# Moving the softmax reciprocals and the near-bias copies from VectorE to GpSimd

## The chip, the cores and the metric

The kernel runs on one core of a Trainium2 chip. A core has five engines with a queue of instructions each: TensorE (PE in the profile; its weight loads are PEld), VectorE (DVE), ScalarE (ACT), GpSimd (POOL) and SyncE (SP), which issues DMA transfers. An engine works through its queue in order. If its next instruction waits for a semaphore, everything behind it waits too.

The metric is the device time of one execution in microseconds, as the median of the runs.

## The reference

Two layers of the same kind, on 1024 positions with 1024 channels. Each layer normalises its input, projects it, runs a convolution branch and a sparse-attention branch side by side, gates both, concatenates them and projects them out. The attention branch is the part that matters here:

```
cq = rmsnorm(c_q); q = (cq @ w_uq) -> 8 heads of 128; kv = rmsnorm(c_kv)      # one kv head for all
score = sum over index heads of w_idx * relu(q_idx @ k_idx)                   # causal
sel = top_k(score, 256)                                                       # keys for each query
logits = q . kv[sel] * 128**-0.5 + rel_bias[bucket(t - s)]
probs = softmax(logits where t - s >= 0)
o = (probs @ kv[sel]) @ w_uv;  y_attn = o * silu(g_attn)
y = concat(y_conv, y_attn) @ w_out;  x = x + gate * rmsnorm(y)
```

Input and output are float32, and TensorE products are made of three passes over high and low parts.

## The kernel before

The kernel doesn't gather the selected keys. It computes the logits of all causal keys and adds a mask with a very large number where a key isn't selected; the mask is the bfloat16 tile mask. The signs are turned: the logits come out of TensorE negated, and Exp is taken with scale −1, so the row maximum of the logits is a row minimum in the code.

The work order of the attention is a list, ORDER, of 16 runs (pr, c). pr is a pair of heads (0 to 3), c a pair of query tiles of 128 rows (0 to 3). A run handles two heads e and two tiles i = 2c, 2c + 1; tile i has 128 (i + 1) keys. There are 64 such tiles in a layer, 128 in all. One tile passes through these steps:

1. TensorE: logits lg (L116 to L118) into one of four PSUM buffers.
2. GpSimd: the near bias plus the mask into the last 256 columns of p (L846). For the tiles i < 2, where no key is masked but those of the future, there is no sum: GpSimd makes the causal triangle of the last 128 columns (L843, an affine_select), and for i = 1 a plain copy of the bias fills the 128 columns before (L842). The bias tile tb is ja or jv for some heads.
3. VectorE: lg plus the bias or the mask into p, with the row minimum mx in the same instruction (L852, L856).
4. ScalarE: Exp on p, with its row sum into ri[:, 0] (L859).
5. The reciprocal of the sum into ri[:, 1] (L860).
6. The scaling of p by it: on ScalarE (L862) for the runs of pr 0 and for (1, 0), 20 tiles of a layer, on GpSimd (L864) for the other 44.
7. For c < 3, TensorE transposes p into PSUM (pt, L877), and ScalarE (L882) and VectorE (L884) copy the result to SBUF in turn. For c = 3, VectorE transposes blocks (stage, L895) and DMAs through DRAM do the rest (pd, L898 and L907).
8. TensorE: value products av (L927); VectorE multiplies by the gate (L918).

p has five buffers (tag t4). A new tile's first writer on p (L842, L843 or L846) therefore waits until the transposes or the stage of the tile five before have read it.

The selection runs into the start of the attention: select(j) makes the mask of one of the six tiles with more than 256 keys. Its steps are a compare with count (L614), the number still needed (L616), an equality (L618), a scan (L619) and a product (L620) on VectorE, a sum on GpSimd (L621, gt) and the scaled mask on ScalarE (L622). The table SELECT places four of the six between runs of the first pairs.

The end of the attention carries other work: the loads of the output projection's weights (DMA raw, ScalarE woh L136, GpSimd wol L137) and the splitting of the attention's result into yh (ScalarE L993) and yl (VectorE or GpSimd, L994). Output projection matmuls o (L116 to L118) follow, some of them ahead of the last value products.

A scheduler with its own plan of durations fixes the order in which each engine gets its instructions; some edges are set by hand (issue_after). The order can therefore change in places that the edit doesn't touch.

The GpSimd instruction that the change uses exists elsewhere: L301 and L1051 compute x to the power −0.5 with tensor_tensor and op pow, against a tile mhalf of −0.5.

Of the kernel before, what the change touches and what calls it, by code (L numbers as in the profile page):

```python
# [11 lines left out]
F32 = mybir.dt.float32  # L12
# [7 lines left out]
OP = mybir.AluOpType  # L20
# [3 lines left out]
P = 128  # L24
# [56 lines left out]
def hybrid_kernel(ctx: ExitStack, tc: tile.TileContext, x, cT, w_ada, w_mod, bcol, bgate, g_pre, w_in, w_cp,  # L81
# [3 lines left out]
    V, S, G, T = nc.vector, nc.scalar, nc.gpsimd, nc.tensor  # L85

    cst = ctx.enter_context(tc.tile_pool(name="cst", bufs=1))
# [14 lines left out]
    def st(tag, shape, dt=F32, name=None, bufs=None):  # L102
        return sb.tile(shape, dt, name=name or tag, tag=tag, bufs=bufs or BUFS.get(tag, 1))
# [7 lines left out]
    def lg_ps(name="lg"):  # L111
        return ps.tile([P, 512], F32, name=name, tag="lg", bufs=4)

    def mm3(o, a, b, first, last):
        (ah, al), (bh, bl) = a, b
        T.matmul(o, ah, bh, start=first, stop=False)  # L116
        T.matmul(o, ah, bl, start=False, stop=False)  # L117
        return T.matmul(o, al, bh, start=False, stop=last)  # L118
# [28 lines left out]
    make_identity(nc, ident)  # L147
    mhalf = cst.tile([P, 16], F32, name="mhalf")
    V.memset(mhalf, -0.5)
    kc1 = cst.tile([P, 6], F32, name="kc1")  # L150
    kc2 = cst.tile([P, 6], F32, name="kc2")
    for j in range(6):
# [151 lines left out]
    def pieces(i):  # L304

        w = P * (i + 1)
        if i == 4:
            return [(0, 384), (384, 640)]
        return [(c, min(c + 512, w)) for c in range(0, w, 512)]
# [497 lines left out]
    def attention(l, cq, kv, v, mk, sga, wq, select, yc):  # L807
# [19 lines left out]
        def probs(q, tb_, i, early):  # L827

            w = P * (i + 1)
            o = []  # L830
            for c0, c1 in pieces(i):
                o.append((lg_ps("lg"), c0, c1))
                mark[2] = mm3(o[-1][0][:, :c1 - c0], tuple(x_[:, 128 * i:128 * i + 128] for x_ in q),
                              tuple(x_[:, c0:c1] for x_ in kv), True, True)
            n0 = max(0, w - 256)
            nw = w - n0
            tb = tb_[:, 256 - nw:]
            p = st("t4", [P, 1024], name="p")
            nb = p[:, n0:w]
            if i < 2:  # L840
                if nw > 128:
                    V.tensor_copy(nb[:, 0:nw - 128], tb[:, 0:nw - 128])  # L842
                G.affine_select(nb[:, nw - 128:nw], tb[:, nw - 128:nw], pattern=[[-1, P]],  # L843
                                compare_op=OP.is_ge, fill=BIG, base=0, channel_multiplier=1)
            else:
                G.tensor_tensor(nb, tb, mk[:, OFF[i] + n0:OFF[i] + w], op=OP.add)  # L846
            m = st("mx", [P, 3], name="mx", bufs=8)
            lo = FMAX
            for o_, c0, c1 in o:
                if c0 < n0:  # L850
                    e = min(c1, n0)
                    V.tensor_tensor_reduce(out=p[:, c0:e], in0=o_[:, :e - c0], in1=mk[:, OFF[i] + c0:OFF[i] + e],  # L852
                                           scale=1.0, scalar=lo, op0=OP.add, op1=OP.min,
                                           accum_out=m[:, c0 // 384:c0 // 384 + 1])
                    lo = m[:, c0 // 384:c0 // 384 + 1]
            mark[3] = V.tensor_tensor_reduce(out=nb, in0=o_[:, n0 - c0:w - c0], in1=nb, scale=1.0, scalar=lo,  # L856
                                             op0=OP.add, op1=OP.min, accum_out=m[:, 2:3])
            ri = st("ri", [P, 2], name="ri", bufs=8)
            mark[0] = S.activation(p[:, :w], p[:, :w], AF.Exp, scale=-1.0, bias=m[:, 2:3], accum_out=ri[:, 0:1])  # L859
            V.reciprocal(ri[:, 1:2], ri[:, 0:1])  # L860
            if early:
                S.activation(p[:, :w], p[:, :w], AF.Copy, scale=ri[:, 1:2])  # L862
            else:
                mark[1] = G.tensor_scalar(p[:, :w], p[:, :w], ri[:, 1:2], 1.0, op0=OP.mult, op1=OP.mult)  # L864
            return p
# [65 lines left out]
        def run(pr, c):  # L931

            if c == 3:
                if "pd" not in held:
                    held["pd"] = st("score", [P, 4, 2, 4, 4, 32], name="pd")
                pts = [[held["pd"][:, 2 * e + h] for h in range(2)] for e in range(2)]
            else:
                pts = [[st("hq", [P, 4, 256], name="pt") for _ in range(1 + c // 2)] for e in range(2)]
            for e in range(2):
                for ii in range(2):  # L940
                    i = 2 * c + ii
                    p = probs(*q[2 * pr + e], i, pr == 0 or (pr, c) == (1, 0))
                    if c == 3:
                        turned(p, ii, pts[e])
                    else:
                        transposed(p, i, ii, pts[e])
                for j in SELECT.get((pr, c, e), ()):
                    with tc.issue_after(mark[3].ins):
                        select(j)
            if back:  # L950
                back.pop()()
            for w in open_:
                w[0] += c + 1
            if open_ and open_[0][0] >= 3:
                values(*open_.pop(0)[1], mark[2])
            if c == 3:
                open_.append([0, (pr, c, pts)])
            else:
                values(pr, c, pts)
# [351 lines left out]
```

## Time and profile before

| | |
|---|---|
| median of 3 runs | 1219.5 us (1219.34 to 1225.55) |
| profiled execution, its own time | 1223.55 us |
| its span, first to last instruction | 1221.8 us |
| mean granted TensorE clock | 0.984 of full speed |
| TensorE busy | 1151.2 us, 94% |
| VectorE busy | 910.9 us, 75% |
| ScalarE busy | 704.4 us, 58% |
| GpSimd busy | 567.1 us, 46% |

The profiled execution is 4.05 us above the median, and 1.75 us of it lie around the span. Times below are from the span's start. The attention of layer 0 lies at about 360 to 540 us, that of layer 1 at about 950 to 1130 us.

How to read the views: a busy row of a stretch gives how long each engine worked in it. A row of waits names the engine and line that waited, behind the arrow the engine, tile and line whose end released it, then the total, the number of times and the longest. A timeline row gives start and duration, engine, line and operation, out<-in with shapes, and in brackets how long the engine had been idle before it and what ended that. Matmuls overlap, so a TensorE row's duration is longer than its share of the pace.

### The profile page before, as it was taken

To read this page: it belongs to the slowest core of one execution; us is meant where nothing else is said; L and a number is where in the kernel's file an instruction comes from. 1 tells how busy PE (TensorE), PEld (TensorE's weight loads), DVE (VectorE), ACT (ScalarE), POOL (GpSimd) and SP (SyncE) were. 2 spreads that over 40 slices of the span, in tenths; PEclk is the share of its full clock that TensorE was granted. 3 is DMA by queue.
4 is the path that set the end of the run, shared out by engine and by line. 5 is a ranking of instruction groups with operands and counts; after the bars stand their busy time and mean duration, and the time that the engine had idled before them with its cause. 6 is when DMAs were issued, how large, how long until landed. Compare 5 with 4: busy or idle time off the path is not lost. (4 is left out here: it accounts for less than half of the span.)

```text
span 1221.8 us, 23105 instructions
## 1 busy us (share of the span) xinstructions
PE 1151.2 (94%) x7592; PEld 954.0 (78%) x7592; DVE 910.9 (75%) x2214; ACT 704.4 (58%) x1624; POOL 567.1 (46%) x1178
## 2 busy tenths in 40 slices
PE   6999999999998799999999999999999788998998
PEld 3788888877875467689988888888788566676997
DVE  4667798898877778857686588898888888777315
ACT  4545767766875645552354457786577575466221
POOL 3441226547543355664492411454665345576322
PEclk9999999999998999999999999999999898999999
DMA  9630258852110155658761220986111005567205
GB/s 351 206 86 18 69 178 268 278 195 79 34 38 1 24 156 155 186 195 264 262 212 31 57 52 20 288 293 198 55 36 45 9 1 139 138 162 217 89 18 190
DMA packets 145384, 161.68 MB, mean 132 GB/s; under 512 B 63080, under 2 KB 116848, under 8 KB 145264
## 3 DMA queue, kind: packets, MB, share of 16 engines
q1 hardware_dynamic: 145264, 160.21, 42.9%
q8 instruction: 60, 0.98, 0.4%
q14 instruction: 60, 0.49, 0.1%
HBM read 130.79 MB, written 29.37 MB: 131 GB/s over the span
## 5 line engine op out<-in xcount | busy, mean ns | idle before, releaser
L563 DVE TENSOR_SCALAR_CACHE_REDUCE jv<-pl,cand 128x768 int8<-128x768 uint16 (+1 forms) x186 | 187.9, 1010 | 31.6 <-POOL cand L570 20.7
L558 ACT ACTIVATE ja<-pl,cand 128x896 int8<-128x896 uint16 (+1 forms) x186 | 154.2, 829 | 63.9 <-POOL cand L570 49.3
L859 ACT ACTIVATE p<-p,mx 128x128 f32<-128x128 f32 (+7 forms) x128 | 98.3, 770 | 62.3 <-DVE mx L856 59.9
L116 PE MATMUL o<-woh,yh 128*128 128x256 f32 x384 | 109.1, 286 | 0.2 <-DVE mx L856 0.2
L117 PE MATMUL o<-wol,yh 128*128 128x256 f32 x384 | 108.0, 283 | 0.0
L118 PE MATMUL o<-woh,yl 128*128 128x256 f32 x384 | 107.6, 283 | 0.0
L137 POOL TENSOR_TENSOR wul<-raw,wuh 128x342 fp32r<-128x342 f32 (+1 forms) x48 | 47.0, 1003 | 129.6 <-ACT wuh L136 123.5
L116 PE MATMUL u<-hT,wuh 128*128 128x512 f32 x256 | 101.4, 396 | 0.0
L116 PE MATMUL g<-hT,wgh 128*128 128x512 f32 x256 | 101.2, 395 | 0.0
L118 PE MATMUL u<-hT,wul 128*128 128x512 f32 x256 | 100.0, 391 | 0.0
L117 PE MATMUL u<-hT,wuh 128*128 128x512 f32 x256 | 100.0, 391 | 0.0
L117 PE MATMUL g<-hT,wgh 128*128 128x512 f32 x256 | 99.8, 390 | 0.0
L118 PE MATMUL g<-hT,wgl 128*128 128x512 f32 x256 | 99.7, 390 | 0.0
L494 DVE SCALAR_TENSOR_TENSOR score<-relu,widx,score 128x384 f32<-128x384 f32 (+2 forms) x84 | 78.9, 977 | 18.7 <-ACT relu L486 18.1
L486 ACT ACTIVATE relu<-ixs 128x512 f32<-128x512 f32 (+2 forms) x140 | 66.7, 523 | 35.9 <-PE ixs L480 35.4
L864 POOL TENSOR_SCALAR p<-p,ri 128x384 f32<-128x384 f32 (+3 forms) x88 | 67.8, 777 | 37.1 <-DVE ri L860 36.8
L1036 ACT ACTIVATE ja<-o 128x256 int8<-128x256 f32 x64 | 24.5, 383 | 99.3 <-PE o L118 99.3
L480 PE MATMUL ixs<-ix 128*128 128x512 f32 (+2 forms) x320 | 76.3, 356 | 0.5 <-ACT relu L486 0.5
L116 PEld LDWEIGHTS o<-woh,yh 128*128 128x128 f32 x384 | 73.1, 191 | 2.4 <-issue 1.2
L117 PEld LDWEIGHTS o<-wol,yh 128*128 128x128 f32 x384 | 73.3, 191 | 0.3 <-issue 0.3
L118 PEld LDWEIGHTS o<-woh,yl 128*128 128x128 f32 x384 | 72.9, 191 | 0.0
L927 PE MATMUL av<-pt,v 128*64 128x256 f32 (+1 forms) x384 | 61.0, 371 | 9.1 <-DVE pt L884 5.3
(312 smaller groups left out, 3460.4 us busy)
## 6 DMA issues: line engine op xcount, KB each, us to landing
wt<-in_wl_dram SPq DMA_DIRECT2D x64, 512.0 KB, 6.0
wa<-in_w_mod_dram SPq DMA_DIRECT2D x32, 512.0 KB, 4.8
pd<-stage SPq DMA_DIRECT2D x192, 64.0 KB, 1.9
pd<-pd SPq DMA_DIRECT2D x48, 256.0 KB, 3.1
raw<-in_w_in_dram SPq DMA_DIRECT2D x64, 171.0 KB, 2.6
wa<-in_w_ada_dram SPq DMA_DIRECT2D x16, 512.0 KB, 10.1
raw<-in_w_out_dram SPq DMA_DIRECT2D x32, 171.0 KB, 3.5
raw<-in_w_in_dram SPq DMA_DIRECT2D x32, 170.0 KB, 2.6
```

Source lines behind the costliest of these rows:

```text
L116: T.matmul(o, ah, bh, start=first, stop=False)
L117: T.matmul(o, ah, bl, start=False, stop=False)
L118: return T.matmul(o, al, bh, start=False, stop=last)
L137: eng.tensor_tensor(lo[:, c:e], raw[:, :e - c], f32(hi[:, c:e]), op=OP.subtract)
L480: mark = T.matmul(o[:, :c1 - c0], s_[:, 128 * i:128 * i + 128], ix[:, kk, c0:c1], start=kk == 0, stop=kk == 1)
L486: S.activation(r[:, c0:c1], o[:, :c1 - c0], AF.Relu)
L494: V.scalar_tensor_tensor(acc, r[:, :w], wc, acc, op0=OP.mult, op1=OP.add)
L558: S.activation(ja[:, :wid(j)], src, AF.Sign, scale=-1.0, bias=col(cand, c), accum_out=col(ct_, c))
L563: V.tensor_scalar(jv[:, :wid(j)], src, col(cand, c), None, op0=OP.is_lt, op1=OP.add, accum_out=col(ct_, c))
L859: mark[0] = S.activation(p[:, :w], p[:, :w], AF.Exp, scale=-1.0, bias=m[:, 2:3], accum_out=ri[:, 0:1])
L864: mark[1] = G.tensor_scalar(p[:, :w], p[:, :w], ri[:, 1:2], 1.0, op0=OP.mult, op1=OP.mult)
L927: T.matmul(o[64 * e:64 * e + 64, 128 * ii:256], lh, pt[:, ii:2, :, j % 4, :] if c == 3 else pt[:, j % 4, 128 * ii:256], start=j == 0, stop ...
```

## The change

A constant tile mone, 128x1 with −1.0, is set once on VectorE. The copy L842 and the reciprocal L860 are issued on GpSimd; the reciprocal becomes x to the power −1, a tensor_tensor with op pow against mone. The steps before and after them stay where they are. New line numbers are two higher.

```diff
     mhalf = cst.tile([P, 16], F32, name="mhalf")
     V.memset(mhalf, -0.5)
+    mone = cst.tile([P, 1], F32, name="mone")
+    V.memset(mone, -1.0)
...
             if i < 2:
                 if nw > 128:
-                    V.tensor_copy(nb[:, 0:nw - 128], tb[:, 0:nw - 128])
+                    G.tensor_copy(nb[:, 0:nw - 128], tb[:, 0:nw - 128])
                 G.affine_select(nb[:, nw - 128:nw], tb[:, nw - 128:nw], pattern=[[-1, P]],
                                 compare_op=OP.is_ge, fill=BIG, base=0, channel_multiplier=1)
...
             mark[0] = S.activation(p[:, :w], p[:, :w], AF.Exp, scale=-1.0, bias=m[:, 2:3], accum_out=ri[:, 0:1])
-            V.reciprocal(ri[:, 1:2], ri[:, 0:1])
+            G.tensor_tensor(ri[:, 1:2], ri[:, 0:1], mone[:, 0:1], op=OP.pow)
```

128 reciprocals and 16 copies change engines. Because the scheduler plans anew, other instructions move as well. In the orders below each row is an instruction with line, operation, tiles and shape.

VectorE in the early stretch of layer 0, before, around the near-bias copy of p<-jv and the selects of 640 and 768 columns:

```order
L842 COPY p<-ja 128x128
L860 RECIPROCAL ri<-ri 128x1
L884 COPY pt<-pt 128x2x128
L860 RECIPROCAL ri<-ri 128x1
L842 COPY p<-jv 128x128
L614 TENSOR_SCALAR gt,cnt<-score,tf 128x640
L618 TENSOR_SCALAR eq<-score,tf 128x640
L614 TENSOR_SCALAR gt,cnt<-score,tf 128x768
L884 COPY pt<-pt 128x2x128
L618 TENSOR_SCALAR eq<-score,tf 128x768
L820 SCALAR_TENSOR_TENSOR q_4534<-uq,q_4533 128x512
```

The same place after the change (L616 is the old L614, L620 the old L618, L886 the old L884):

```order
L886 COPY pt<-pt 128x2x128
L616 TENSOR_SCALAR gt,cnt<-score,tf 128x640
L620 TENSOR_SCALAR eq<-score,tf 128x640
L616 TENSOR_SCALAR gt,cnt<-score,tf 128x768
L620 TENSOR_SCALAR eq<-score,tf 128x768
L886 COPY pt<-pt 128x2x128
L822 SCALAR_TENSOR_TENSOR q_4536<-uq,q_4535 128x512
```

The compares and equalities of both selects now follow the first copy of pt directly, and both equalities stand ahead of the second.

GpSimd in the same stretch, before, from the sums of the selects of 384 and 512 columns on:

```order
L621 TENSOR_TENSOR gt<-gt,eq 128x384
L621 TENSOR_TENSOR gt<-gt,eq 128x512
L843 AFFINE_SELECT p<-ja 128x128
L843 AFFINE_SELECT p<-jv 128x128 x2
L846 TENSOR_TENSOR p<-tb,mask 128x256
L621 TENSOR_TENSOR gt<-gt,eq 128x640
L621 TENSOR_TENSOR gt<-gt,eq 128x768
L846 TENSOR_TENSOR p<-tb,mask 128x256 x7
```

GpSimd there after the change (L623 is the old L621, L845 the old L843, L848 the old L846; L862 is the new reciprocal, L844 the moved copy):

```order
L862 TENSOR_TENSOR ri<-ri,mone 128x1 x2
L844 COPY p<-ja 128x128
L845 AFFINE_SELECT p<-ja 128x128
L862 TENSOR_TENSOR ri<-ri,mone 128x1
L845 AFFINE_SELECT p<-jv 128x128
L862 TENSOR_TENSOR ri<-ri,mone 128x1
L844 COPY p<-jv 128x128
L845 AFFINE_SELECT p<-jv 128x128
L848 TENSOR_TENSOR p<-tb,mask 128x256
L623 TENSOR_TENSOR gt<-gt,eq 128x640
L623 TENSOR_TENSOR gt<-gt,eq 128x768
L862 TENSOR_TENSOR ri<-ri,mone 128x1 x2
```

Each tile's reciprocal now stands in this queue; those of two tiles come behind the sums of 640 and 768 columns.

GpSimd at the end of the attention of layer 0, before, from the second-last causal triangle to the first loads of the output projection (wol and wo are weight splits, yl the splits of the attention's result):

```order
L843 AFFINE_SELECT p<-jv 128x128
L137 TENSOR_TENSOR wol<-raw,woh 128x340
L843 AFFINE_SELECT p<-jv 128x128
L864 TENSOR_SCALAR p<-p,ri 128x128
L137 TENSOR_TENSOR wol<-raw,woh 128x342 x2
L137 TENSOR_TENSOR wol<-raw,woh 128x340
L864 TENSOR_SCALAR p<-p,ri 128x256
L994 TENSOR_TENSOR yl<-An,yh 128x512 x3
L137 TENSOR_TENSOR wo<-raw,wo 128x342 x2
L137 TENSOR_TENSOR wo<-raw,wo 128x340
```

The same place after the change (L866 is the old L864, L996 the old L994):

```order
L137 TENSOR_TENSOR wol<-raw,woh 128x342 x2
L862 TENSOR_TENSOR ri<-ri,mone 128x1
L137 TENSOR_TENSOR wol<-raw,woh 128x340
L866 TENSOR_SCALAR p<-p,ri 128x256
L844 COPY p<-jv 128x128
L845 AFFINE_SELECT p<-jv 128x128
L866 TENSOR_SCALAR p<-p,ri 128x128
L137 TENSOR_TENSOR wo<-raw,wo 128x342 x2
L996 TENSOR_TENSOR yl<-An,yh 128x512 x3
L137 TENSOR_TENSOR wo<-raw,wo 128x340
L862 TENSOR_TENSOR ri<-ri,mone 128x1
L866 TENSOR_SCALAR p<-p,ri 128x256
```

The last tile's reciprocal and scaling (128x256) came ahead of the three yl subtractions; now they come behind them and behind three wo splits. In TensorE's order 85 o matmuls stood ahead of the last value products of layer 0, and 111 do now; in layer 1 there are 85 in both, and the last scaling stays ahead of yl.

## Rows read from the trace of the kernel before

**Rows 1.** Busy us by stretch: PE, PEld, DVE, ACT, POOL; granted clock; DMA; GB/s.

```profile
361.00:386.00 25.00, 18.13 (x75) 12.73 (x73) 16.00 (x43) 13.33 (x34) 8.58 (x9) 0.86 0.00 1
386.00:411.00 25.00, 20.58 (x121) 14.35 (x122) 23.13 (x73) 17.50 (x38) 7.27 (x10) 1.00 0.00 1
...
484.00:535.00 51.00, 47.91 (x326) 36.05 (x325) 38.35 (x135) 33.38 (x77) 35.37 (x48) 1.00 0.70 195
540.00:640.00 100.00, 99.83 (x818) 96.92 (x816) 69.82 (x92) 38.63 (x113) 58.74 (x83) 1.00 0.71 237
```

**Rows 2.** Waits of all engines, 360 to 535 us.

```profile
ACT p L859 <- DVE mx L856: 32.4, 20, 3.9
```

**Rows 3.** Lines L860 and L842: ns min/median/max; engine idle before, us, times, until.

```profile
L860 DVE RECIPROCAL ri<-ri x128: 119/157/166, 363.0 to 1123.7; 128x1 f32<-128x1 f32 x128
...
  ACT p L859: 17.7, 25
...
L842 DVE COPY p<-tb x8: 188/224/785, 348.2 to 1047.9; 128x128 f32<-128x128 f32 x8
```

**Rows 4.** Timeline of the early stretches: DVE first, then PE and POOL.

```profile
371.64 0.23 DVE L842 COPY p<-jv 128x128 f32<-128x128 f32 x1 [3.87 <-PE pt L877]
...
373.98 0.42 DVE L884 COPY pt<-pt 128x256 f32<-128x256 f32 x1
374.84 0.68 DVE L820 SCALAR_TENSOR_TENSOR q<-uq,q 128x512 fp32r<-128x512 f32 x1
...
381.80 0.36 DVE L860 RECIPROCAL ri<-ri 128x1 f32<-128x1 f32 x2
...
387.55 0.16 DVE L860 RECIPROCAL ri<-ri 128x1 f32<-128x1 f32 x1
387.62 0.47 DVE L856 CUSTOM_DVE_ANT_0 p<-lg,p,mx 128x256 f32<-128x256 f32 x1
...
966.62 0.23 DVE L842 COPY p<-jv 128x128 f32<-128x128 f32 x1 [3.10 <-PE pt L877]
...
371.33 0.49 PE L877 MATMUL pt<-ident,p 128*128 128x128 f32 x3
374.54 1.51 PE L927 MATMUL av<-pt,v 128*64 128x256 f32 x6 [1.64 <-DVE pt L884]
...
379.94 3.99 POOL L621 TENSOR_TENSOR gt<-gt,eq 128x640 f32<-128x640 f32 x2 [7.29 <-DVE eq L620]
```

**Rows 5.** Waits of DVE, 360 to 386 us.

```profile
DVE ri L860 <- ACT p L859: 1.5, 2, 0.8
```

**Rows 6.** Lines L301 and L843: engine, operation, times, ns min/median/max.

```profile
L301 POOL TENSOR_TENSOR rx<-rxv,mhalf x16: 548/554/1037, 8.1 to 639.3; 128x1 f32<-128x1 f32 x16
...
L843 POOL TENSOR_SCALAR_AFFINE_SELECT p<-tb x16: 283/292/565, 335.9 to 1048.0; 128x128 f32<-128x128 f32 x16
```

**Rows 7.** Line L860 (361 to 411, 484 to 535); waits of POOL (484 to 535).

```profile
L860 DVE RECIPROCAL ri<-ri x16: 149/158/166, 363.0 to 405.8; 128x1 f32<-128x1 f32 x16
...
L860 DVE RECIPROCAL ri<-ri x21: 122/156/165, 484.0 to 531.3; 128x1 f32<-128x1 f32 x21
...
POOL p L864 <- DVE ri L860: 9.1, 6, 4.6
```

**Rows 8.** Timeline of POOL, then PE, at the end of layer 0's attention.

```profile
532.01 0.48 POOL L864 TENSOR_SCALAR p<-p,ri 128x256 f32<-128x256 f32 x1
533.79 5.12 POOL L994 TENSOR_TENSOR yl<-An,yh 128x512 fp32r<-128x512 f32 x3 [1.29 <-ACT yh L993]
538.87 3.10 POOL L137 TENSOR_TENSOR wo<-raw,wo 128x342 fp32r<-128x342 f32 x3
...
541.67 0.83 PE L927 MATMUL av<-pt,v 128*64 128x256 f32 x6
```

**Rows 9.** Timeline of DVE, then POOL, around 456 us.

```profile
456.16 0.79 DVE L842 COPY p<-tb 128x128 f32<-128x128 f32 x1
...
455.75 1.12 POOL L864 TENSOR_SCALAR p<-p,ri 128x1024 f32<-128x1024 f32 x1 [0.61 <-DVE ri L860]
```

## The prediction

> **What bounds the kernel now.** I read the busy time by stretches first, because the page's shares (TensorE 94%, VectorE 75%) are means over stages with different limits. Only the two attention stages, some 180 us each, hold lines L842 and L860, so only there can the change act directly; the reader should look for stretches where TensorE has holes. Its first 50 us have them: TensorE is busy 18.13 and 20.58 of 25 us in layer 0, while VectorE is busy 23.13 of the second 25 [rows 1]; layer 1 repeats the pattern. So the start of attention is set by VectorE, together with the waits between engines. The last 51 us are the other way round: TensorE is busy 47.91, VectorE 38.35, GpSimd 35.37. The waits of all engines say the same: the longest sum in layer 0 is ScalarE's Exp waiting for VectorE's row maximum, 32.4 us [rows 2]. Where GpSimd waits for reciprocals, they are therefore late because VectorE's queue is full, not because one takes long (157 ns median) [rows 3].
>
> **What is taken from VectorE.** There are three terms.
>
> *The copy that blocks.* In both layers one near-bias copy (L842, i = 1) stands at the head of VectorE's queue and waits for a free p buffer, which TensorE's transposes release: 3.87 us at 371.64 and 3.10 us at 966.62 [rows 4]. Behind it stand the select's compares, which need nothing from it, as the order shows. After the change the copy waits on GpSimd, ahead of an affine_select that waits for the same buffer (the order before has it on GpSimd already), so there the wait costs nothing new. What is late next on VectorE is the second L884 copy, whose transposes end at 371.33 + 0.49 = 371.82; before it ran at 373.98. L820 behind it then starts at about 371.9 + 0.33 = 372.2, not 374.84: 2.6 of the 3.87 us are won. TensorE had waited 1.64 us at 374.54 for exactly that L884, so it sees this. Layer 1 in proportion: 3.10 × 2.6 / 3.87 = 2.1. Sum 4.7; ends 0 and 3.87 + 3.10 = 7.0.
>
> *Issue time of the reciprocals.* One reciprocal holds VectorE for 0.07 us (387.55 to the next start, 387.62) [rows 4] up to its 0.16 [rows 3]. Sixteen start between 361 and 411 us [rows 7], where VectorE has little slack: 16 × 0.07 = 1.1 us a layer, upper end 2.6. I take the lower, since instructions overlap wherever the next has its inputs. Sum 2.2.
>
> *Waits of reciprocals for Exp.* VectorE stood idle 17.7 us (25 times) until an Exp had ended [rows 3]. All of it is gone, but only where VectorE sets the pace does it come back as time. I take the row of the first 26 us of attention, 1.5 us [rows 5], for each layer: 3.0, ends 0 and about 9 (half of all).
>
> Gains together: 4.7 + 2.2 + 3.0 = 9.9 us.
>
> **What is put on GpSimd.** No pow on a softmax sum is in the trace, but the same instruction on another 128x1 tile is: 554 ns median (L301) [rows 6], 3.5 times the reciprocal. 128 of them are 71 us, and 16 copies at the nearest row of that shape, an affine_select of 292 ns, are 4.7 us: GpSimd goes from 567 to 643 us busy. Three places decide whether it shows.
>
> *Late stretch (484 to 535, and 1076 to 1127).* 21 reciprocals [rows 7] and 2 copies fall here: 21 × 0.554 + 2 × 0.292 = 12.2, so 35.37 + 12.2 = 47.6 of 51 us. Of today's idle 15.6 us, 9.1 are waits for reciprocals [rows 7], which turn into the pow itself; the other 6.5 are waits for other engines. 47.6 + 6.5 = 54.1: 3.1 us too much a layer, if no wait shrinks. If TensorE, busy 47.91, sets the end all the same, it is 0. I take the middle, 1.5 a layer: 3.0.
>
> *The last tile of layer 0.* Its reciprocal now stands behind the three L994 subtractions and one split of a weight load; the subtractions end at 533.79 + 5.12 = 538.9, and a split takes a third of 3.10 [rows 8], so with that and the pow its scaling slips from 532.0 to about 540.5. What covers this: TensorE's order now has 111 output-projection matmuls ahead of the last value product instead of 85, and 26 × 99.83 / 818 = 3.2 us by the pace of the stretch from 540 to 640 [rows 1], while that product ran only at 541.67 [rows 8]. It is due at about 544.9, and the chain from 540.5 (scaling 0.48 [rows 8], then transpose and copy) has 3.9 us left for what follows the scaling. Cost 0; without the cover, up to 5.
>
> *Behind the select's additions.* In the early stretch the reciprocals of two tiles now stand behind L621 for 640 and 768 columns (3.99 us for both [rows 4], waiting for VectorE's eq). VectorE gets to eq 2.6 us sooner, so the additions end at about 383.9 − 2.6 = 381.3, and the two pows at 382.4, against 382.2 for the reciprocals today [rows 4]. Cost 0, with up to 2 us a layer if eq doesn't come sooner. Here the same exchange is at its clearest: a wait that blocked VectorE now blocks softmax sums.
>
> **A shared port.** In one row a VectorE L842 copy takes 0.79 us, where its shortest takes 0.188 [rows 3]; a GpSimd scaling of 1.12 us began 0.41 us ahead of it and ended with it [rows 9]. More GpSimd instructions of half a microsecond could thus hold up VectorE. The Trainium skill, page "SBUF — State Buffer", section "Who interferes with whom", has this as a rule: the two engines share a pair of SBUF ports, as an exclusive lock that the first holds for its whole instruction, against VectorE's copies and against its operations with two SBUF inputs. The trace agrees in that row (0.79 against 0.19). As a mechanism of this kernel: 16 pows a layer in the early stretch, each stopping half of what it meets for half its length, 16 × 0.5 × 0.28 = 2.2 us a layer. It is the third rival below.
>
> **Sum.** −9.9 + 3.0 = −6.9 us: span 1221.8 to 1214.9, execution 1223.55 to 1216.65. The profiled execution is 4.05 us above the median of the runs, 1219.5, so the median becomes 1212.6.
>
> **Rivals.**
> *Slower: GpSimd becomes the bound of the late stretch.* GpSimd works in order, and a pow waits for its Exp just as the scaling waited for the reciprocal. If half of the 9.1 us stays as waits for Exp, the stretch needs 54.1 + 4.6 = 58.7 us, 7.7 more a layer; and if half of the early gain is lost on the way (2.4 left of 4.9 a layer), the net is +5.3 a layer: 1219.5 + 10.6 = 1230. It decides from the point at which GpSimd's work and waits there exceed 51 us by more than the early gain of 4.9. For it: a load of 47.6 in 51 us by the sum above, and the 9.1 us of waiting into the scaling today. Against: five p buffers let GpSimd run late by a tile, and TensorE has output projection to fill with.
> *Within the measurement: what the start gains, the end gives back.* Late stretch 3.1 and the select's queue 1 cost 4.1 of 4.9 a layer: 1219.5 − 1.6 = 1217.9. For it: the late stretch has TensorE at 47.91 of 51, so it can take little; against: TensorE's holes of the first 50 us are real and are not refilled later.
> *The shared port takes it.* 2.2 a layer off the 3.4 net: 1219.5 − 2.4 = 1217.1. For it the row of 0.79 us; against: a pow reads one column of 128 elements, and nothing shows how long it holds anything.
> That the change does nothing can't be: in the new order VectorE has no L842 and no L860, GpSimd all 144.
>
> **How the numbers follow.** About 0.5%, 6 us, is what a measurement of this kernel can tell from no change: faster is below 1213.4, slower above 1225.6. Chances: forecast 0.46 (its own range 1201 to 1215: the ends of the gains reach further down than the cost's ends reach up; 0.41 of it below 1213.4), GpSimd the bound 0.23 (about all above 1225.6), given back 0.22, port 0.09. That makes faster 0.41, same 0.36, slower 0.23. Range: low, 1219.5 less 7.0, 5.2 and 6 is 1201; high, the slower rival reaches 1230, of which half is left out: 1229.
>
> **What would show it.** Right: no VectorE idle of 3 us at the two copies, and L614 for 640 columns some 4 us sooner after the copy of pt; TensorE's busy share up and its holes smaller in the first 50 us of attention; Exp's wait for the row maximum below 32.4 us; pow rows near 0.55 us; GpSimd near 47 of 51 us at the end, with attention ending 3 to 4 us sooner a layer. Wrong: TensorE's transposes or value products waiting for GpSimd scaling in the late stretch (rival one); the select's masks late (rival two); VectorE's copies and selects longer than before (rival three). What would make it wrong outright is a pow that takes 0.7 to 1.0 us on softmax sums, or a GpSimd queue with another blocked head that I haven't seen.

## The result: slower by half a percent, where a gain of seven microseconds was forecast

| | before | after |
|---|---|---|
| median of 12 runs each | 1220.01 us | 1228.14 us |
| ratio | | 1.0056 (95% interval 1.0043 to 1.007) |
| span of the profiled execution | 1221.8 us | 1223.3 us |
| VectorE busy | 910.9 us | 895.5 us |
| GpSimd busy | 567.1 us | 642.7 us |

The forecast was 1212.6 us, faster. The kernel became slower by 6.9 us by the ratio (5.2 to 8.5), which is what the text below goes by; the two medians lie 8.1 apart. The time lies in the range, and near the first rival, to which the prediction gave 0.23. The profiled execution after took 1225.03 us, 3.1 below its median, and the one before lay above its own. So the two traces show 1.5 us of a loss that the runs put at 6.9. Where the lead turns can still be read in them.

The busy time by stretch of the kernel after (columns as in [rows 1]: PE, PEld, DVE, ACT, POOL, granted clock, DMA share, GB/s):

```profile
361.00:386.00 25.00, 19.39 (x82) 13.37 (x80) 16.47 (x44) 14.58 (x38) 13.41 (x19) 0.86 0.00 1
386.00:411.00 25.00, 21.17 (x117) 14.18 (x118) 21.28 (x55) 17.31 (x35) 14.64 (x18) 0.93 0.00 1
484.00:535.00 51.00, 44.70 (x294) 32.47 (x292) 33.78 (x105) 31.81 (x71) 44.62 (x66) 0.97 0.65 184
...
540.00:640.00 100.00, 100.00 (x822) 97.38 (x822) 68.77 (x91) 38.08 (x112) 57.02 (x81) 1.00 0.70 233
1076.00:1127.00 51.00, 44.84 (x286) 33.31 (x286) 32.37 (x101) 30.87 (x70) 45.75 (x68) 0.93 0.64 183
```

Against [rows 1], the first 25 us of attention do what was forecast for TensorE: it works more (19.39 us instead of 18.13, 82 matmuls instead of 75). In the second 25 it is busy longer (21.17 instead of 20.58), but at a granted clock of 0.93 instead of 1.00, and does 117 matmuls instead of 121. VectorE has less to do over the two (37.75 us instead of 39.13). The last 51 us do the opposite: GpSimd is busy 44.62 us instead of 35.37, and TensorE falls from 47.91 to 44.70.

The waits of all engines after, 360 to 535 us (total, times, longest):

```profile
ACT p L861 <- DVE mx L858: 35.4, 21, 5.2
...
POOL ri L862 <- ACT p L861: 15.0, 14, 2.4
...
PE pt L879 <- POOL p L866: 8.6, 4, 2.9
```

and the last of these in the kernel before:

```profile
PE pt L877 <- POOL p L864: 1.3, 1, 1.3
```

TensorE's transposes now wait 8.6 us for GpSimd's scaling, where it was 1.3. This is the row that the prediction named for its first rival. It isn't the measure of the loss, though. Of the 8.6 us, 4.2 lie at 423 to 425 us, well ahead of the place where the lead goes, and the same 4.2 stand there in a kernel below that loses nothing (reciprocals of the first 11 runs on GpSimd). TensorE's waits from 360 to 470 us, after and in that kernel, then after from 470 to 541:

```profile
PE pt L879 <- POOL p L866: 4.2, 2, 2.9
```

```profile
PE pt L882 <- POOL p L869: 4.2, 2, 2.9
```

```profile
PE pt L879 <- POOL p L866: 4.3, 2, 2.9
```

In the last stretch of layer 1 (1060 to 1130 us) there is no such wait. Exp's wait for the row maximum didn't shrink, as the forecast had it, but is 35.4 instead of 32.4 [rows 2].

The longest wait of the last stretch in the timeline of TensorE after, two of the matmuls behind it, and the stretches around it:

```profile
513.07 1.11 PE L879 MATMUL pt<-ident,p 128*128 128x128 f32 x4 [2.91 <-POOL p L866]
...
514.62 0.63 PE L116 MATMUL lg<-kvT,qx 128*128 128x512 f32 x1
515.04 0.63 PE L117 MATMUL lg<-kvT,qx 128*128 128x512 f32 x1
```

```profile
508.00:512.00 4.00, 2.02 (x13) 1.70 (x13) 2.91 (x8) 2.63 (x6) 3.90 (x6) 1.00 0.58 144
512.00:514.00 2.00, 0.93 (x5) 0.94 (x6) 2.00 (x6) 0.59 (x2) 2.00 (x3) 0.71 1.01 310
514.00:516.00 2.00, 2.00 (x7) 1.28 (x6) 2.00 (x7) 1.44 (x4) 1.83 (x4) 0.50 0.38 98
516.00:518.00 2.00, 2.00 (x9) 1.06 (x9) 2.00 (x4) 0.15 (x2) 1.76 (x3) 0.93 0.68 161
```

Matmuls of the same shape in the kernel before, close by:

```profile
511.22 0.40 PE L116 MATMUL lg<-kvT,qx 128*128 128x512 f32 x1
511.46 0.39 PE L117 MATMUL lg<-kvT,qx 128*128 128x512 f32 x1
```

GpSimd is busy 3.90 of 4.00 and 2.00 of 2.00 us around TensorE's hole. Behind the hole the granted clock is 0.50, the lower of its two levels, for some 3 us, and matmuls of 512 columns start 0.42 us apart there, against 0.24 before. So the hole costs more than its length.

Where the lead is won and lost can be read tile by tile. The table gives the mean start of Exp (L859, in the later kernels L861) of the four tiles of a run, minus that of the same tiles before, worked out from the timelines; minus is earlier. Runs are counted from 0 in the order of ORDER. The profiled execution before lay 3.5 us above its median of 12, so leads read a little large; what counts is how they change. The last column is the mean time from the end of Exp to the end of the scaling over the 20 tiles of runs 11 to 15.

| kernel | layer 0, run 1 | run 10 | run 15 | layer 1, run 1 | run 10 | run 15 | Exp to scaled, layers 0, 1 |
|---|---|---|---|---|---|---|---|
| before | | | | | | | 2.58, 2.92 us |
| after | −2.0 | −3.2 | +1.7 | −2.3 | −4.5 | +0.9 | 3.90, 4.08 |
| copies alone | −3.2 | −3.7 | −0.3 | −7.2 | −8.6 | −7.3 | 3.40, 3.09 |
| first 11 runs | −3.2 | −5.0 | −4.3 | −7.3 | −7.4 | −6.5 | 3.06, 3.12 |
| last 5 runs | −2.2 | −3.8 | +2.1 | +0.5 | −0.8 | +6.9 | 4.38, 4.39 |
| last 5 runs, doubled | −3.0 | −4.5 | +9.3 | 0.0 | −0.2 | +17.3 | 6.66, 6.82 |
| mult for pow | −1.8 | −6.9 | −6.8 | −8.4 | −12.5 | −10.3 | 2.29, 2.53 |
| relief | −2.6 | −3.2 | −3.6 | −7.6 | −6.4 | −5.2 | 2.85, 2.87 |

After the change the kernel leads by 3.2 us until run 10 of layer 0, and has lost 4.9 by run 15; in layer 1 it loses 5.4. From run 11 on the lead goes. A change of some 3 us can also be the order's doing: the copies alone lose 3.4 between run 10 and run 15 of layer 0, all of it in run 15 (−3.9 at run 14), and only 1.3 in layer 1.

### The profile page after: what moved, and what is told of

Its sections match the earlier page's. It is cut to its first block, busy times and chain, and to the rows that moved or that the text cites. A ratio compares the mean times of both kernels' runs of the same rounds, so it can differ in the third digit from the quotient of the medians.

```text
span 1223.3 us, 23157 instructions
## 1 busy us (share of the span) xinstructions
PE 1153.3 (94%) x7592; PEld 954.5 (78%) x7592; DVE 895.5 (73%) x2071; ACT 704.5 (58%) x1624; POOL 642.7 (53%) x1322
## 5 line engine op out<-in xcount | busy, mean ns | idle before, releaser
L861 ACT ACTIVATE p<-p,mx 128x128 f32<-128x128 f32 (+7 forms) x128 | 98.3, 769 | 67.4 <-DVE mx L858 67.2
L862 POOL TENSOR_TENSOR ri<-ri,mone 128x1 f32<-128x1 f32 x128 | 74.8, 590 | 27.4 <-ACT p L861 24.4
L488 ACT ACTIVATE relu<-ixs 128x512 f32<-128x512 f32 (+2 forms) x140 | 66.7, 523 | 35.9 <-PE ixs L482 35.4
L879 PE MATMUL pt<-ident,p 128*128 128x128 f32 x336 | 59.1, 292 | 22.3 <-POOL p L866 12.8
```

What stands on the lines that cost most here:

```text
L488: S.activation(r[:, c0:c1], o[:, :c1 - c0], AF.Relu)
L862: G.tensor_tensor(ri[:, 1:2], ri[:, 0:1], mone[:, 0:1], op=OP.pow)
L879: T.transpose(t[:, 128 * j:128 * j + 128], p[:, 128 * (j0 + j):128 * (j0 + j) + 128], ident)
```

## The experiments

**Theory:** the early stretch gains, as forecast; from run 11 on GpSimd's queue is so full that each pow delays the scalings behind it, and TensorE waits for them. **Rivals:** the scheduler's new order costs, whatever is moved; the longer way from Exp over GpSimd to the scaling costs wherever it stands; the select's sums ahead of early reciprocals cost. All ratios are to runs of before on the same chip, with 95% intervals.

### One half of the change at a time

Copies on GpSimd, reciprocals back on VectorE:

```diff
-            G.tensor_tensor(ri[:, 1:2], ri[:, 0:1], mone[:, 0:1], op=OP.pow)
+            V.reciprocal(ri[:, 1:2], ri[:, 0:1])
```

> Only the 16 near-bias copies are on GpSimd; the 128 reciprocals are back on VectorE. Theory (VectorE's blocked head gives time early, GpSimd's queue takes it late): the copy's blocked head (3.87 and 3.10 us before) goes, so Exp of the runs 1 to 3 starts 1.5 to 2 us earlier in each layer, and nothing is lost late, since GpSimd gets only 2 copies (0.6 us) there: ratio to before 0.997 to 0.999, about 1217. Rival (the new plan's order costs, whatever is moved): ratio 1.003 or more here too.

Measured: **0.9965** (0.9951 to 0.9979), 1216.7 us, just below the band. The copies alone gain 4.3 us. Most of the lead is there at run 1: 2.5 us come from run 0 to run 1 in layer 0, 4.5 in layer 1 (−2.7 to −7.2). In layer 1 it holds to the end, in layer 0 to run 14. This kernel has a new order as well, and it costs nothing on the whole. VectorE's timeline of this kernel at the place of [rows 4]:

```profile
366.96 0.15 DVE L862 RECIPROCAL ri<-ri 128x1 f32<-128x1 f32 x1
367.03 0.86 DVE L616 TENSOR_SCALAR_CACHE_REDUCE gt<-score,tf 128x640 f32<-128x640 f32 x1
...
371.33 0.42 DVE L886 COPY pt<-pt 128x256 f32<-128x256 f32 x1 [1.50 <-PE pt L879]
371.67 0.68 DVE L822 SCALAR_TENSOR_TENSOR q<-uq,q 128x512 fp32r<-128x512 f32 x1
```

and GpSimd's copy there:

```profile
370.94 0.29 POOL L844 COPY p<-jv 128x128 f32<-128x128 f32 x1 [3.95 <-PE pt L879]
```

The select starts at 367.03 instead of 371.78, and the wait of 3.95 us stands on GpSimd, where it blocks nothing that is late.

Reciprocals on GpSimd, copies back on VectorE:

```diff
-                    G.tensor_copy(nb[:, 0:nw - 128], tb[:, 0:nw - 128])
+                    V.tensor_copy(nb[:, 0:nw - 128], tb[:, 0:nw - 128])
```

> Only the 128 reciprocals are on GpSimd; the copies are back on VectorE. Theory: the late cost is all of the reciprocals', and the copy's early gain is missing: GpSimd busy 44 to 45 of the last 51 us of attention again, time from an Exp's end to the end of its scaling near 4 us in runs 11 to 15 (2.6 before), ratio 1.006 to 1.010. Rival (the copies do the harm): ratio below 1.002.

Measured: **1.0066** (1.0046 to 1.0085). All of the loss is the reciprocals'. The two halves don't add up: −0.0035 and +0.0066 make +0.0031, and the whole has +0.0056. The three intervals leave room for that.

### Early and late reciprocals

```diff
-            G.tensor_tensor(ri[:, 1:2], ri[:, 0:1], mone[:, 0:1], op=OP.pow)
+            if early:
+                G.tensor_tensor(ri[:, 1:2], ri[:, 0:1], mone[:, 0:1], op=OP.pow)
+            else:
+                V.reciprocal(ri[:, 1:2], ri[:, 0:1])
```

> Copies on GpSimd, and the reciprocals of the 20 tiles of a layer that ScalarE scales (runs 0 to 4); the 44 whose scaling is on GpSimd have VectorE's reciprocal again. Theory: the early gain of 2 to 5 us a layer stays, the late cost goes (GpSimd 35 to 36 of 51 us late): ratio 0.993 to 0.997, 1211 to 1216. Rival (early reciprocals on GpSimd gain nothing; all the gain is the copies'): the ratio of the copies alone. Rival (the order costs): 1.003 or more.

Measured: **0.9979** (0.9966 to 0.9992). The loss is gone, as expected, but the ratio misses the forecast band by 0.0009: the early reciprocals gain nothing beside the copies.

The counterpart has the two branches exchanged and the copies on VectorE:

> Only the 44 reciprocals of a layer whose scaling is on GpSimd (runs 5 to 15) are on GpSimd; early reciprocals and all copies on VectorE. Theory: the late cost in full and no early gain: ratio 1.008 to 1.013, slower than the changed kernel itself. Rival (the early reciprocals, behind the select's sums, do the harm): ratio 1.000 to 1.003.

Measured: **1.011** (1.0089 to 1.0132). As expected, the 44 late reciprocals of a layer carry the loss. That this is more than with the 20 early ones moved as well (1.0066) isn't explained; each kernel has an order of its own, and no run here holds the order fixed.

The next two split at run 11, where GpSimd's stretch becomes dense. Both have the copies on GpSimd.

```diff
-        def probs(q, tb_, i, early):
+        def probs(q, tb_, i, early, last):
...
-            G.tensor_tensor(ri[:, 1:2], ri[:, 0:1], mone[:, 0:1], op=OP.pow)
+            if last:
+                V.reciprocal(ri[:, 1:2], ri[:, 0:1])
+            else:
+                G.tensor_tensor(ri[:, 1:2], ri[:, 0:1], mone[:, 0:1], op=OP.pow)
...
-                    p = probs(*q[2 * pr + e], i, pr == 0 or (pr, c) == (1, 0))
+                    p = probs(*q[2 * pr + e], i, pr == 0 or (pr, c) == (1, 0), ORDER.index((pr, c)) > 10)
```

> Copies on GpSimd; reciprocals on GpSimd for the first 11 runs of ORDER, on VectorE for the last 5. Theory (GpSimd's queue is the bound from run 11 on, and only there): the cost goes, ratio 0.996 to 0.999, and Exp's lead over before is kept through runs 11 to 15. Rival (a reciprocal on GpSimd costs wherever it stands, by its longer way from Exp to scaling): 24 of 44 late ones still pay, ratio 1.001 to 1.005.

Measured: **0.9969** (0.9957 to 0.9982). 88 of the 128 reciprocals on GpSimd cost nothing against the copies alone.

With the branches exchanged, only the last five runs' 40 reciprocals are on GpSimd:

> Copies on GpSimd; reciprocals on GpSimd only for the last 5 runs of ORDER (20 of 64 tiles a layer). Theory: the copies' gain (0.9965) and all of the late cost (4 to 9 us a layer): ratio 1.003 to 1.009. Rival (the cost is spread over all reciprocals): 20/44 of it, ratio 0.999 to 1.002.

Measured: **1.0071** (1.0055 to 1.0086). These 40 carry the whole loss: 1.0071 − 0.9965 = 0.0106, 12.9 us, 6.5 a layer. The late stretch of the two, first with the first 11 runs' on GpSimd, then with the last 5's:

```profile
484.00:535.00 51.00, 46.18 (x318) 35.04 (x317) 36.49 (x123) 31.47 (x73) 32.91 (x46) 0.97 0.64 188
1076.00:1127.00 51.00, 47.62 (x337) 36.31 (x336) 37.59 (x123) 30.10 (x71) 34.98 (x47) 1.00 0.67 201
```

```profile
484.00:535.00 51.00, 44.37 (x283) 30.59 (x282) 32.70 (x102) 30.61 (x68) 45.96 (x68) 0.97 0.63 182
1076.00:1127.00 51.00, 46.24 (x280) 34.27 (x280) 33.46 (x107) 29.82 (x65) 44.64 (x66) 0.90 0.61 178
```

GpSimd has 45.96 and 44.64 us of work instead of 32.91 and 34.98, and TensorE does 283 and 280 matmuls in the stretch instead of 318 and 337. Its busy time says less: at a granted clock of 0.90, 46.24 us of busy time are fewer matmuls. The windows are fixed, and at run 15 the first kernel is ahead of the second by 6.4 and 13.4 us, so they don't hold quite the same work.

TensorE's own wait for GpSimd's scaling is short in the kernel that has the loss (470 to 541, then 1060 to 1140 us):

```profile
PE pt L882 <- POOL p L869: 1.6, 1, 1.6
```

```profile
PE pt L882 <- POOL p L869: 0.7, 1, 0.7
```

So the load on GpSimd makes the loss, but this one wait carries only a part of it. Through which others it reaches TensorE isn't shown.

### More and less of the same load

Twice the pows in the last five runs:

```diff
-            ri = st("ri", [P, 2], name="ri", bufs=8)
+            ri = st("ri", [P, 3], name="ri", bufs=8)
...
-            G.tensor_tensor(ri[:, 1:2], ri[:, 0:1], mone[:, 0:1], op=OP.pow)
+            if last:
+                G.tensor_tensor(ri[:, 2:3], ri[:, 0:1], mone[:, 0:1], op=OP.pow)
+                G.tensor_tensor(ri[:, 1:2], ri[:, 0:1], mone[:, 0:1], op=OP.pow)
+            else:
+                V.reciprocal(ri[:, 1:2], ri[:, 0:1])
```

> As the kernel with the reciprocals of the last 5 runs on GpSimd (1.0071), but with each of these 20 pows a layer issued twice (the first into a column that nothing reads). Theory (GpSimd's queue is the bound there, so its work counts in full): 20 × 0.56 = 11 us more a layer, of which half to all shows: ratio 1.016 to 1.025. Rival (the cost is that of the place in the queue or of the new order, not of the load): ratio 1.006 to 1.010.

Measured: **1.017** (1.0141 to 1.0198). The first 40 pows are 22 us of GpSimd's time (40 × 0.55) and cost 12.9; the second 40 cost another 12.1 (1.017 − 1.0071). The load counts at somewhat over half, both times alike. In layer 0 the stretch is now filled (50.38 of 51 us), in layer 1 GpSimd is busy 44.70, as with single pows, but its last scaling ends at 1147.4 us instead of 1137.7. TensorE's clock is down in both:

```profile
484.00:535.00 51.00, 42.82 (x252) 29.37 (x252) 30.84 (x94) 27.73 (x60) 50.38 (x78) 0.87 0.57 165
1076.00:1127.00 51.00, 38.84 (x223) 28.07 (x222) 34.50 (x99) 26.46 (x59) 44.70 (x68) 0.87 0.59 169
```

The other way, a shorter instruction in the place of pow. It multiplies the sum by −1, so p is scaled by minus the sum and the kernel leaves out the reciprocal; only its time is of use:

```diff
-            G.tensor_tensor(ri[:, 1:2], ri[:, 0:1], mone[:, 0:1], op=OP.pow)
+            G.tensor_tensor(ri[:, 1:2], ri[:, 0:1], mone[:, 0:1], op=OP.mult)
```

> The changed kernel with mult in place of pow, so p is scaled by minus the sum and not by its reciprocal; all else is the same, but the scheduler's order shifts. The instruction should take about 0.2 us, not 0.55 to 0.59. Theory (the load of GpSimd's queue late): 21 × 0.37 = 7.8 us less work in the last 51 us, so GpSimd at 37 to 38 us of 51 and ratio 0.995 to 1.000. Rival (the place in GpSimd's queue, that is waiting in order for Exp, costs, not the length): ratio 1.004 to 1.007.

Measured: **0.9936** (0.992 to 0.9952), below the band. The instruction (ns, minimum, median, maximum) and the late stretches of this kernel:

```profile
L862 POOL TENSOR_TENSOR ri<-ri,mone x128: 179/190/1256, 363.7 to 1120.6; 128x1 f32<-128x1 f32 x128
```

```profile
484.00:535.00 51.00, 48.47 (x339) 36.58 (x338) 37.62 (x105) 31.63 (x74) 39.91 (x68) 1.00 0.70 205
1076.00:1127.00 51.00, 48.16 (x349) 36.73 (x348) 34.88 (x92) 29.75 (x73) 36.38 (x63) 1.00 0.65 196
```

All 128 stand on GpSimd, each behind its Exp, and they take 0.19 instead of 0.55 us. With that the kernel gains 7.8 us of 1221, near the forecast. So it is the length of the instruction on GpSimd that turns a gain of 7.8 us into a loss of 6.9, not the wait for Exp in its queue. The order differs too: compared in sequence, 93 of 1322 instructions of GpSimd, 239 of 2071 of VectorE and 673 of 7592 matmuls stand elsewhere. That it isn't the order rests on the other kernels, which agree. The other values in p don't show in the times: of the 127 other groups (line and shape) of instructions of VectorE, ScalarE and GpSimd after 650 us, all but two (splits yl on VectorE) keep their median duration to 10 ns.

Two more ask where mult gains over the copies alone: mult only in the first 11 runs, then only in the last 5, with VectorE's reciprocal in the others.

> Copies on GpSimd; the first 11 runs have mult in place of pow on GpSimd (p is scaled by minus the sum), the last 5 VectorE's reciprocal. It asks where the 3.5 us lie by which mult everywhere (0.9936) beats the copies alone (0.9965). Theory (VectorE's freed time early is worth something, and pow's 0.35 us more eats it): ratio 0.993 to 0.995. Rival (the gain is late, from VectorE's late stretch): 0.996 to 0.998.

Measured: **0.9943** (0.9925 to 0.9961). Against the copies alone this is 0.0022 less, 2.7 us; the intervals overlap, so it isn't shown.

> The counterpart: copies on GpSimd; VectorE's reciprocal in the first 11 runs, mult in place of pow on GpSimd in the last 5 (p there scaled by minus the sum). Theory (the length of the instruction in GpSimd's late queue is the cost, so 20 × 0.2 = 4 us a layer costs little): ratio 0.995 to 1.000, against 1.0071 with pow. Rival (leaving VectorE late is what gains): 0.993 to 0.995. Rival (any further wait in GpSimd's late queue costs): 1.004 to 1.007.

Measured: **0.9972** (0.9952 to 0.9992). In the last runs 0.19 us costs nothing that can be measured, and gains nothing. With pow the same place costs 12.9 us. So the cost doesn't grow in proportion to the load: 7.6 us of GpSimd's time (40 × 0.19) cost 0.9 us, within the noise, and 22 cost 12.9.

### Other work taken from GpSimd

The whole change, with the low halves of three weight loads on VectorE:

```diff
-        return load_w(w_out[l, g, :, 1024 * j:1024 * j + 1024], 1024, "wo", "pl" if j and g % 2 else "w4")
+        return load_w(w_out[l, g, :, 1024 * j:1024 * j + 1024], 1024, "wo", "pl" if j and g % 2 else "w4", eng=V if g == 0 or (g, j) == (1, 0) else G)
```

> The changed kernel, with the low halves of the output projection's first three weight loads (L137 wol, 9 instructions of about 0.95 us a layer, in the attention's last stretch) on VectorE instead of GpSimd. Theory: GpSimd has some 8 us less to do late and the loss goes: ratio 0.996 to 1.001. Rival (the order, or the chain through pow, costs and not GpSimd's load): ratio 1.004 or more.

Measured: **0.9983** (0.997 to 0.9996). The pows stay on GpSimd, and the loss is gone. The late stretches of this kernel:

```profile
484.00:535.00 51.00, 47.28 (x334) 36.27 (x333) 41.87 (x118) 34.13 (x79) 43.24 (x61) 1.00 0.69 203
1076.00:1127.00 51.00, 46.53 (x327) 35.00 (x326) 40.76 (x112) 31.58 (x72) 43.57 (x61) 1.00 0.65 196
```

GpSimd is nearly as busy in them as after the change (44.62 and 45.75 us), so its busy share of a fixed window doesn't tell what it costs. What differs is what stands ahead of the scalings: here the last one of the layer ends at 529.90 and 1120.40 us, and the remaining 5.10 and 6.60 us of the windows are other work behind it. From Exp to scaled it takes 2.85 and 2.87 us.

The control, the same relief with VectorE's reciprocals:

> Copies on GpSimd, all reciprocals on VectorE, and the low halves of the first three weight loads of the output projection on VectorE instead of GpSimd, as in the kernel with relief (0.9983). Theory (without the reciprocals GpSimd isn't the bound late, so taking work from it gives nothing, and VectorE has 9 instructions more): 0.996 to 0.999, no better than the copies alone. Rival (the relief helps whatever stands in GpSimd's queue, so it proves nothing on the reciprocals): 0.990 to 0.993.

Measured: **0.9994** (0.9978 to 1.0011). This is 0.0004 above the band. Where GpSimd isn't full, the relief gives nothing; the kernel is 3.5 us slower than the copies alone (0.9994 against 0.9965), and that VectorE's added work is what costs them isn't shown. With the relief in both, moving the reciprocals costs nothing that can be measured (0.9983 against 0.9994). So what it repaired was the reciprocals' load on GpSimd's queue.

## Why the prediction failed, step by step

**The copies: right in the sum.** Forecast 4.7 us, measured 4.3. That the sum fits so well is in part luck: in the one trace the lead grows by 2.5 us from run 0 to run 1 of layer 0 (forecast 2.6), but by 4.5 in layer 1 (forecast 2.1), and not all of it reaches the end. The select starts where it should, and L822 starts at 371.67, or 373.02 in the kernel after, against 374.84 before [rows 4]: 1.8 to 3.2 us of the forecast 2.6. In the kernel after, VectorE and GpSimd stand there like this:

```profile
367.49 0.42 DVE L886 COPY pt<-pt 128x256 f32<-128x256 f32 x1 [1.84 <-PE pt L879]
367.83 0.87 DVE L616 TENSOR_SCALAR_CACHE_REDUCE gt<-score,tf 128x640 f32<-128x640 f32 x1
...
372.68 0.42 DVE L886 COPY pt<-pt 128x256 f32<-128x256 f32 x1 [2.04 <-PE pt L879]
373.02 0.68 DVE L822 SCALAR_TENSOR_TENSOR q<-uq,q 128x512 fp32r<-128x512 f32 x1
```

```profile
378.12 3.98 POOL L623 TENSOR_TENSOR gt<-gt,eq 128x640 f32<-128x640 f32 x2 [4.52 <-DVE eq L622]
382.07 1.06 POOL L862 TENSOR_TENSOR ri<-ri,mone 128x1 f32<-128x1 f32 x2
```

What came next to be late was what the prediction named, the transposes ahead of the second copy of pt.

**VectorE's reciprocals: the size was wrong.** Two terms gave 2.2 and 3.0 us. With pow the first 88 gain nothing (0.9969 against 0.9965). With an instruction of 0.19 us they gain about 2.7, and all 128 gain 3.5 (0.9936 against 0.9965). So VectorE's freed time was worth some 3 us, not 5, as far as mult shows it, and pow's own length takes that back. The two pows behind the select's sums are an example: the sums end at 382.10 instead of 383.93, 1.8 us earlier and not 2.6, and the pows at 382.07 + 1.06 = 383.1 where VectorE's reciprocals had ended at 382.2 [rows 4]. The prediction had 382.4 and set the cost at nothing. (In its range the low end takes 6 us for the waits where the text gave about 9; the measured time lies inside either way.)

**pow's price: right.** It takes what L301 had shown [rows 6]; the copy takes the 0.29 us of the affine_select.

```profile
L862 POOL TENSOR_TENSOR ri<-ri,mone x128: 540/550/1510, 363.5 to 1124.4; 128x1 f32<-128x1 f32 x128
```

**The late stretch: the step that failed.** The sum of load was right (47.6 us forecast; the row shows 44.62, in a stretch that no longer holds all of the work). From 54.1 us of work and waits in 51, and 0 if TensorE sets the end, the prediction took the middle, 1.5 us a layer, 3.0 in all. The kernel with the last 5 runs' on GpSimd shows 6.5 a layer, 12.9 in all, against the copies alone. Two things were missing. First, the bound asked only whether GpSimd's work *fits* into the stretch. But a queue that isn't full yet can make each scaling wait: with the last 5 runs' on GpSimd it takes 4.4 us from the end of Exp to the end of the scaling, instead of 2.6 to 2.9 before and 3.1 to 3.4 with the copies alone. Each tile passes that queue three times, with its bias, its pow and its scaling. Second, TensorE's own load doesn't hide this: its queue is in order too, so a late transpose stops the matmuls behind it, for 4.3 us in the last stretch of layer 0. That isn't the whole way to the loss. Layer 1 loses as much without such a wait, and the last 5 runs' pows cost 6.5 a layer with 1.6 and 0.7 us of it. That GpSimd's load is the cause is shown by mult, by the doubled pows and by the relief; which waits pass the rest on stays open. The first rival had the right mechanism, and a size of 5.3 net a layer where 3.5 was measured (6.9 / 2). Its load and its waits came from rows, the halves that it took of them did not; but the middle value came from no row either and had no better claim to the larger chance. Summed up, −4.3 for the copies, about nothing for the first 88 reciprocals and 12.9 for the last 40 make 8.6, where the whole change shows 6.9; the rest isn't explained.

**The last tile of layer 0: right.** Its scaling did slip behind yl and began at 540.98 (forecast 540.5), and TensorE's other matmuls covered it: busy 100.00 of 100 us from 540 on, with the last value products at 546.48.

```profile
534.00 5.13 POOL L996 TENSOR_TENSOR yl<-An,yh 128x512 fp32r<-128x512 f32 x3 [1.32 <-DVE yl L996]
539.10 1.08 POOL L137 TENSOR_TENSOR wo<-raw,wo 128x340 fp32r<-128x340 f32 x1
540.15 0.73 POOL L862 TENSOR_TENSOR ri<-ri,mone 128x1 f32<-128x1 f32 x1
540.98 0.48 POOL L866 TENSOR_SCALAR p<-p,ri 128x256 f32<-128x256 f32 x1
```

**The shared port: it shows the other way round.** The third rival would make VectorE's copies and selects longer. The copy of pt takes 449 ns in the mean before and 451 after; it reads PSUM, while the copy of [rows 9] reads SBUF, so it isn't the same case. The scan takes 1616 and 1650 ns, and the difference is one scan of 2.71 us that met a bias sum on GpSimd, not a pow:

```profile
403.84 0.67 POOL L848 TENSOR_TENSOR p<-tb,mask 128x256 f32<-128x256 f32 x1 [0.17 <-ACT mask L624]
...
403.94 2.71 DVE L621 TENSOR_TENSOR_SCAN score<-eq 128x1024 f32<-128x1024 f32 x1
```

What became longer are pows. Ten of the 128 take 0.73 to 1.51 us instead of 0.55, 5.0 us more in all. Each of them overlaps an equality, a scan or a product of the select, or a split yl, on VectorE, and ends within 0.42 us behind it, as here:

```profile
395.30 2.02 DVE L621 TENSOR_TENSOR_SCAN score<-eq 128x896 f32<-128x896 f32 x1
...
396.17 1.48 POOL L862 TENSOR_TENSOR ri<-ri,mone 128x1 f32<-128x1 f32 x1 [1.81 <-ACT p L861]
```

The Trainium skill, page "SBUF — State Buffer", section "Who interferes with whom", says that whichever engine issues first gets the shared pair for its whole instruction while the other blocks. Seven of the ten pows agree, since VectorE's instruction had begun first; the other three began 0.13 to 0.30 us ahead of the equality that they overlap. Only three of the ten lie behind run 11's start, with 0.9 us, so this isn't the late loss.

**Given back: half right.** The second rival's picture, a gain at the start that the end returns, is what the table shows for the kernel after; only it returns more than it got.

## What to carry to other kernels

Before moving small work to a helper engine, take its load in the densest stretch, not its share of the span: GpSimd's 46% were 69% in the last 51 us of attention, and pows that took it to 87% cost over half of their length. But the share alone doesn't settle it: with the weight splits taken away it was 85% in the same window, and nothing was lost. In the table, the kernels that lose late take 3.9 us and more from Exp to the scaled tile, the others 3.4 and less. Look first for the instruction that blocks a queue while it waits: moving 16 copies gained 4.3 us, moving 128 reciprocals lost all of it and more. The version to keep is the one with the copies alone (1216.7 us, 0.9965), faster than both kernels here.

## What the runs showed of the hardware

On a 128x1 tile GpSimd's tensor_tensor takes 0.19 us with mult and 0.55 with pow (medians of 128 each), so pow adds 0.36 us on this tile. VectorE's reciprocal of the same tile takes 0.157. The Trainium skill, page "GPSIMD Engine Reference", section "3.1 Elementwise — side-by-side cycle accounting", gives GpSimd about half of VectorE's speed for an add on large tiles. Here pow takes 3.5 times the reciprocal, and mult only 1.2 times: the operation makes the difference.
